# One joint tile for the rounded and low activations, and a 512-column matmul in the second mixer's gate

## The chip, the cores and the metric

The kernel runs on one NeuronCore of a Trainium2 chip. The metric is device time in microseconds (us) of one execution. The engines are named as in the profile: PE is TensorE's matmul unit and PEld its weight loads, DVE is VectorE, ACT is ScalarE, POOL is GpSimd, and SP is the queue that issues most of the DMAs.

## The reference

Two layers over 256 tokens of width 2048. The first is an RWKV-7 mixer, the second an attention mixer with three branches (compressed, selected, windowed) of 16 heads. What the change touches is the second mixer's output gate: the last 2048 columns of its input projection, z, go through silu and multiply the attention's result ahead of the output projection.

```python
def nsa_mixer(u, shared, w_in, gate_b, w_o):
    proj = u @ w_in
    q = rope_partial(proj[..., :NSA_WIDTH].reshape(B, T, H, d), jnp.arange(T))
    gl = proj[..., NSA_WIDTH:NSA_WIDTH + N_BRANCH * H] + gate_b
    z = proj[..., NSA_WIDTH + N_BRANCH * H:]
...
    o = o * jax.nn.silu(z)
    return o @ w_o
```

Here u is the RMS-normed hidden state. Weights and activations are float32.

## The kernel before, in words

Every large product is made of three matmuls on rounded numbers. A float32 tensor is split in two: a high part, rounded to fp32r by an ACT copy, and a low part, the remainder, by a subtraction. The product is high by high, high by low and low by high, all summed in one PSUM bank.

**Activations.** The activations are kept transposed, as 16 blocks k of 128 channels by T = 256 tokens. The function `ring` hands out the two tiles of a block, `mh` (high) and `ml` (low), from two rings of 16 slots each; ring 0 serves v, k, y and ob, ring 1 serves w, a, z, r and u. Each pair is written by ACT (high) and DVE or POOL (low): in `split_into` for the first mixer's mixed inputs, in `turn_y` for its result, in `turn_h` for u, and in `flush` for ob, the gated attention result. The dictionary `mixed` maps (name, k) to the pair.

**Weights.** The class `Weights` loads them in pieces of 512 KB (`wraw`, five buffers) through the SP queue, and splits them into units of 128x512: ACT writes `whi` (L204), DVE or POOL writes `wlo` (L189). Of the last 144 units of the second mixer's input projection, every third low half is POOL's. When a unit is taken, the next three have been split as well (`AHEAD` is 3).

**Two kinds of products.** In `rows_step` (L567, L568, L570) the activations are the stationary operand and up to 512 weight columns stream past; it serves v, z, the projections' outputs, the keys and values, and the queries. In `cols_step` (L585 to L587) 128 weight columns are stationary and the 256 tokens of a block stream past, so that the result is transposed, with channels on the partitions; it serves the first mixer's keys and receptance (`phase_k`, `stream`), its low-rank inputs, and the second mixer's gate. A step of k is three matmuls of 256 columns:

```python
PE.matmul(o, wh[:, s, :], mh, start=k == 0 and first, stop=False, **kw)
PE.matmul(o, wh[:, s, :], ml, start=False, stop=False, **kw)
PE.matmul(o, wl[:, s, :], mh, start=False, stop=k == NK - 1, **kw)
```

**The second mixer's stage.** The list `QZ` orders 5 blocks of queries (`phase_q`) and 16 gate heads (`phase_z`, the second function of that name). A gate head runs `cols_block` over 16 blocks k into half a PSUM bank (three banks in turn), then DVE multiplies the sum by `RST`, the row's reciprocal norm, into `zT` (L1461), ACT takes a tanh (L1463), and DVE makes silu's value out of it (L1464). Beside it runs attention as a background generator (`attn_all`, `attend`, `weigh`), a pair of heads at a time: scores, softmax on DVE and ACT, transposes of the probabilities on PE (L232 is the line of the helper that gives attention's matmuls a priority), and the products with the values. ACT copies a pair's result to `og` (L1580, one buffer); `flush` multiplies it by `zT` on POOL (L1594) and splits it into `ob` (L1596 on ACT, L1597 on POOL).

**After it.** `phase_bo` is the output projection. Its first block of 512 columns takes the blocks of `ob` downwards, k = 15 first, in `rows_step`. `open_fin` then releases the attention's memory and loads the final gain (L1622) and the residual (L1624) over the SP queue; `accumulate` (L1630) uses them after the first block.

**Order.** The program's order comes from the generators and their costs in ns (`Sched`). A scheduler then orders each engine's queue by a timeline and places the semaphore waits by the tiles' readers and writers. The start of the kernel and the recurrent scan are written out by hand in a fixed order instead.

Of the kernel before, what the change touches and what calls it, by code (L numbers as in the profile page):

```python
# [11 lines left out]
F32R = mybir.dt.float32r  # L12
AF = mybir.ActivationFunctionType
OP = mybir.AluOpType
AX = mybir.AxisListType
PSUM = bass.MemoryType.PSUM

T, D, NK = 256, 2048, 16
# [197 lines left out]
def hybrid_kernel(ctx: ExitStack, tc: tile.TileContext, a: dict, out: bass.AP):  # L216
    nc = tc.nc
    V, S, G, PE = nc.vector, nc.scalar, nc.gpsimd, nc.tensor
# [35 lines left out]
    def accp(name="acc"):  # L254
        n = turn.get(name, 0)
        turn[name] = n + 1
        b = role[name]
        return psum.tile([128, 512], F32, name=f"bank{b[n % len(b)]}", bufs=1)
# [26 lines left out]
    for q in range(4):  # L285
        for k in (4 * q, 4 * q + 2):
            first, second = [W.add(wv[(k + i) * 128:(k + i + 1) * 128, 0:1024].rearrange("p (u c) -> p u c", u=2), 1, False)
                             for i in range(2)]
# [46 lines left out]
    mixp = ctx.enter_context(tc.tile_pool(name="mixp", bufs=1))  # L335
# [63 lines left out]

    RINGS = {"v": 0, "k": 0, "y": 0, "ob": 0, "w": 1, "a": 1, "z": 1, "r": 1, "u": 1}  # L400
    owners = ([], [])
    used = set()

    def ring(nm, k):
        i = RINGS[nm]
        h = mixp.tile([128, T], F32R, name=f"mh{i}", bufs=NK)
        l = mixp.tile([128, T], F32R, name=f"ml{i}", bufs=NK)
        owners[i].append((nm, k))
        return h, l

    def ring_free(nm):
        o = owners[RINGS[nm]]
# [2 lines left out]
    def split_into(src, nm, k):  # L415
        h, l = ring(nm, k)
        S.activation(h, src, AF.Copy)  # L417
        V.tensor_tensor(l, src, h.bitcast(F32), op=OP.subtract)  # L418
        mixed[(nm, k)] = (h, l)

    def mixed_in(nm, k):
        m = ph1.tile([128, T], F32, name="mtmp", bufs=3)
        mu = MU[{"r": 0, "k": 1, "v": 2, "z": 3, "w": 4, "a": 5}[nm]]
        V.scalar_tensor_tensor(m, xx[:, k, :], mu[:, k:k + 1], xn[:, k, 1:], op0=OP.mult, op1=OP.add)  # L424
        return m
# [34 lines left out]
    if True:  # L460
# [28 lines left out]
        for k in range(2):  # L489
            norm_x(k, px[:, 256 * k:256 * k + 256], V)  # L490
            m = mixed_in("v", k)
# [64 lines left out]
    def need(key):  # L556
        if key not in mixed:
            sch.require(lambda: key in mixed)
        return mixed[key]
# [20 lines left out]
    def cols_step(o, nm, q, first=True, **kw):  # L580
        wh, wl = W.get()
        for s in range(4):
            k = 4 * q + s
            mh, ml = need((nm, k))
            PE.matmul(o, wh[:, s, :], mh, start=k == 0 and first, stop=False, **kw)  # L585
            PE.matmul(o, wh[:, s, :], ml, start=False, stop=False, **kw)  # L586
            PE.matmul(o, wl[:, s, :], mh, start=False, stop=k == NK - 1, **kw)  # L587
            yield 3 * N256

    def cols_block(nm, o):  # L590
        for q in range(4):
            yield from cols_step(o, nm, q)
# [10 lines left out]
    def phase_v():  # L603
        ps = [two() for _ in range(3)]
        lo = accp("lora")
        for q in range(4):
            for k in range(4 * q, 4 * q + 4):
                for nb in ((0, 1, 2), (2, 0, 1))[k % 2]:
                    yield from rows_step(ps[nb], "v", k, W.get(), 512)
            for i, nm in enumerate(("w", "a")):  # L610
                yield from cols_step(lo[:LORA, i * T:(i + 1) * T], nm, q, first=i == 0, skip_group_check=True)
                used.update((nm, k) for k in range(4 * q, 4 * q + 4))
        S.activation(hw, lo[:LORA, 0:T], AF.Tanh)
        S.activation(ha, lo[:LORA, T:], AF.Copy)
        for nb in range(3):
            store_v(nb, ps[nb])
        ps = two()
        yield from rows_block(ps, "v", 512, last=True)
        store_v(3, ps)
        phase_done.add("v")  # L620
# [4 lines left out]
    def phase_z(nb):  # L625
        ps = two()
        yield from rows_block(ps, "z", 512)
        for tt in range(2):
            th = kph.tile([128, 512], F32, name="zth", bufs=2)
            S.activation(th, ps[tt], AF.Tanh, scale=0.5)  # L630
            S.activation(th, th, AF.Copy, scale=0.5, bias=0.5)
            V.tensor_tensor(th, ps[tt], th, op=OP.mult)
            store_heads(zd, nb, tt, th, nc.sync)
# [255 lines left out]
    for nm, i in ZK:  # L889
        sch.run((phase_z3() if i == 3 else phase_z(i)) if nm == "z" else phase_k(i))  # L890
# [213 lines left out]
    def turn_y(U):  # L1104
        yt = [PBK[U][:, x * 512:x * 512 + 256] for x in range(2)]
        for i in range(NCH):
            for x, h in each:
                r = H(x, h)
                PE.matmul(yt[x][R[h], i * 64:i * 64 + 64], OU[U][r, x, i, :], ident[r, r], start=True, **mm)
        made = [ring("y", 2 * U + x) for x in range(2)]  # L1110
        for x, (yh, yl) in enumerate(made):
            S.activation(yh, yt[x], AF.Copy)
            mixed[("y", 2 * U + x)] = (yh, yl)
        for x, (yh, yl) in enumerate(made):
            V.tensor_tensor(yl, yt[x], yh.bitcast(F32), op=OP.subtract)
        sch.t += 350
# [137 lines left out]
    def turn_h(nb, xl):  # L1254
        for kp in range(2):
            pt = accp("tp")
            for i in range(2):
                for tt in range(2):
                    PE.transpose(pt[:, i * 256 + tt * 128:i * 256 + tt * 128 + 128],
                                 xl[:, tt, (2 * kp + i) * 128:(2 * kp + i + 1) * 128], ident)  # L1260
            sch.t += 430
            for i in range(2):
                k = nb * 4 + 2 * kp + i
                src = pt[:, i * 256:i * 256 + 256]
                for nm, gg in (("kv", KVG), ("u", BG)):
                    if nm == "u":
                        h, l = ring(nm, k)
                    else:
                        h = kvp.tile([128, T], F32R, name="kvh", bufs=NK)
                        l = kvp.tile([128, T], F32R, name="kvl", bufs=NK)  # L1270
                    S.activation(h, src, AF.Copy, scale=gg[:, k:k + 1])
                    V.scalar_tensor_tensor(l, src, gg[:, k:k + 1], h.bitcast(F32), op0=OP.mult, op1=OP.subtract)
                    mixed[(nm, k)] = (h, l)
# [146 lines left out]
    RST = at.tile([128, T], F32, name="RST")  # L1420
# [33 lines left out]
            qd[h0 + g] = (qh, ql)  # L1454

    def phase_z(h):
        o = accp("acc")[:, :T]
        yield from cols_block("u", o)
        sch.require(lambda: h + ZB >= HEADS or ("ob", h + ZB) in mixed)
        z = at.tile([128, T], F32, name="zT", bufs=ZB)  # L1460
        V.tensor_tensor(z, o, RST, op=OP.mult)  # L1461
        th = at.tile([128, T], F32, name="zth", bufs=2)
        S.activation(th, z, AF.Tanh, scale=0.5)  # L1463
        V.scalar_tensor_tensor(z, th, 1.0, z, op0=OP.add, op1=OP.mult)  # L1464
        zdone[h] = z
# [146 lines left out]
    for ph in QZ:  # L1612
        sch.run(phase_q(ph) if ph < 10 else phase_z(ph - 10))
# [91 lines left out]
```

## Time and profile before

| | us |
|---|---|
| median of 3 runs | 1187.53 |
| lowest, highest run | 1182.65, 1189.38 |
| span of the profiled execution, first to last instruction | 1181.0 |
| second mixer's stage, queries, attention and gate | 855 to 1087 |
| output projection and final norm | 1087 to 1181 |

The profile gives the profiled execution's span, not its whole time; the median of the runs lies 6.5 us above that span. In the profile's rows "x16" is a count, the number behind the bar is the busy time in us and then the mean duration of one in ns, and the part behind the second bar is the engine's idle time ahead of the group with what ended it. An output and its inputs stand as out<-in. In the rows in order of time the first number is the start and the second the duration, both in us. Matmuls overlap each other, so their durations add up to more than the time they take.

### The profile page before, as it was taken

Reading aid. Unit: us, or ns where it says so; the run is one execution under the profiler, and the core shown is the slowest. Engines: PE = TensorE matmul, PEld = TensorE weight load, DVE = VectorE, ACT = ScalarE, POOL = GpSimd, SP = SyncE. Lnnn points to the kernel's source line nnn. Section 1 sums busy time; section 2 is a strip of 40 time slices with the busy share of each in tenths; the row PEclk is TensorE's granted clock in tenths of the full one; section 3 lists DMA queues with packets and bytes.
Section 4 is the critical chain, followed back from the end, with each engine's and each line's share of the span. In section 5 each row is a group of like instructions: output and inputs, shape, how many; then the busy total and the mean of one; then the engine's idle time right before and its main releaser. Section 6 shows DMA issues by size and latency. Waiting matters only on the chain.

```text
span 1181.0 us, 25607 instructions
## 1 busy us (share of the span) xinstructions
PE 1130.3 (96%) x9416; PEld 985.4 (83%) x9416; DVE 851.3 (72%) x1915; ACT 710.8 (60%) x1680; POOL 330.9 (28%) x413
## 2 busy tenths in 40 slices
PE   8999999999986999999989999999999999999997
PEld 7788899887965888888668888787989989989887
DVE  6999876589794876666655867674576888786564
ACT  5767777666762345565445867564656657665553
POOL 1300046234454255654000010100333233333011
PEclk8999999999997999999999999999999999999999
DMA  6558887786888669685355758585645353644752
GB/s 227 173 181 256 219 224 227 224 215 187 263 236 190 174 173 262 175 220 152 106 169 206 247 163 294 164 285 164 190 131 157 107 138 112 164 104 160 289 195 105
DMA packets 232765, 225.26 MB, mean 191 GB/s; under 512 B 51344, under 2 KB 180672, under 8 KB 232256
## 3 DMA queue, kind: packets, MB, share of 16 engines
q1 hardware_dynamic: 228000, 219.01, 61.8%
q0 software_dynamic: 4640, 4.62, 1.6%
q8 instruction: 74, 1.21, 0.4%
q14 instruction: 51, 0.42, 0.1%
HBM read 200.48 MB, written 23.10 MB: 189 GB/s over the span
## 4 chain that ended last, share of the span: by engine, by line
PE 76%; DVE 12%; DMA 4%; issue 4%; ACT 3%; POOL 2%; SPq 0%; ACTq 0%; POOLq 0%; DVEq 0%
PE bank L568 12%; PE bank L567 12%; PE bank L570 12%; PE bank L585 8%; PE bank L586 6%; PE bank L587 6%; PE bank L232 5%; DVE wlo L189 4%; PE pair L570 1%; PE pair L567 1%; PE pair L568 1%; DVE mtmp L424 1%; DVE ml L418 1%; PE pair L1046 1%; DVE invX L794 1%
## 5 line engine op out<-in xcount | busy, mean ns | idle before, releaser
L189 DVE TENSOR_TENSOR wlo<-wraw,whi 128x512 fp32r<-128x512 f32 (+2 forms) x616 | 441.9, 730 | 151.4 <-ACT whi L204 149.0
L204 ACT ACTIVATE whi<-wraw 128x512 fp32r<-128x512 f32 (+2 forms) x664 | 402.3, 619 | 199.3 <-PE bank L570 96.6
L585 PE MATMUL bank<-mh,whi 128*128 128x256 f32 (+1 forms) x800 | 239.7, 300 | 0.7 <-issue 0.7
L568 PE MATMUL bank<-wlo,mh 128*128 128x512 f32 (+3 forms) x608 | 230.2, 380 | 4.2 <-DVE wlo L189 4.2
L587 PE MATMUL bank<-mh,wlo 128*128 128x256 f32 (+1 forms) x800 | 228.6, 286 | 1.7 <-DVE wlo L189 1.7
L586 PE MATMUL bank<-ml,whi 128*128 128x256 f32 (+1 forms) x800 | 228.7, 286 | 0.0
L570 PE MATMUL bank<-whi,ml 128*128 128x512 f32 (+3 forms) x608 | 228.5, 378 | 0.0
L567 PE MATMUL bank<-whi,mh 128*128 128x512 f32 (+3 forms) x608 | 204.4, 381 | 0.9 <-ACT whi L204 0.9
L585 PEld LDWEIGHTS bank<-mh,whi 128*128 128x128 f32 (+1 forms) x800 | 152.3, 190 | 6.5 <-issue 0.9
L587 PEld LDWEIGHTS bank<-mh,wlo 128*128 128x128 f32 (+1 forms) x800 | 152.3, 191 | 3.2 <-DVE wlo L189 2.0
L586 PEld LDWEIGHTS bank<-ml,whi 128*128 128x128 f32 (+1 forms) x800 | 152.8, 191 | 2.2 <-issue 0.8
L568 PEld LDWEIGHTS bank<-wlo,mh 128*128 128x128 f32 x608 | 115.1, 189 | 22.5 <-DVE wlo L189 5.1
L567 PEld LDWEIGHTS bank<-whi,mh 128*128 128x128 f32 x608 | 114.6, 190 | 20.1 <-ACT whi L204 1.3
L570 PEld LDWEIGHTS bank<-whi,ml 128*128 128x128 f32 x608 | 114.8, 189 | 17.8 <-issue 0.4
L189 POOL TENSOR_TENSOR wlo<-wraw,whi 128x512 fp32r<-128x512 f32 (+2 forms) x48 | 62.6, 1305 | 190.1 <-ACT whi L204 158.3
L568 PE MATMUL bank<-wlo,kvh 128*128 128x512 f32 x192 | 77.0, 401 | 0.0
L570 PE MATMUL bank<-whi,kvl 128*128 128x512 f32 x192 | 76.1, 396 | 0.0
L567 PE MATMUL bank<-whi,kvh 128*128 128x512 f32 x192 | 67.4, 396 | 0.0
L417 ACT ACTIVATE mh<-mtmp 128x256 fp32r<-128x256 f32 x96 | 38.9, 413 | 27.2 <-DVE mtmp L424 25.6
L424 DVE SCALAR_TENSOR_TENSOR mtmp<-xx,prm,xn 128x256 f32<-128x256 f32 x96 | 47.8, 510 | 1.2 <-POOL xx L456 1.0
L715 POOL TENSOR_TENSOR sp<-an,pinv 64x256 f32<-64x256 f32 x32 | 36.3, 1133 | 34.1 <-DVE an L710 32.6
L1035 ACT ACTIVATE X<-pair 128x128 f32<-128x128 f32 x32 | 8.9, 279 | 58.5 <-PE pair L1033 35.9
(325 smaller groups left out, 1909.3 us busy)
## 6 DMA issues: line engine op xcount, KB each, us to landing
wraw<-in_a_w_rkvz_dram SPq DMA_DIRECT2D x128, 512.0 KB, 4.9
wraw<-in_kv_w_dram SPq DMA_DIRECT2D x48, 512.0 KB, 4.5
wraw<-in_b_w_in_dram SPq DMA_DIRECT2D x40, 512.0 KB, 4.0
wraw<-in_a_w_o_dram SPq DMA_DIRECT2D x32, 512.0 KB, 4.1
wraw<-in_b_w_o_dram SPq DMA_DIRECT2D x32, 512.0 KB, 3.7
spd<-sp SPq DMA_DIRECT2D x16, 642.0 KB, 4.7
spl<-spd SPq DMA_DIRECT2D x16, 642.0 KB, 5.6
wraw<-in_b_w_in_dram SPq DMA_DIRECT2D x24, 384.0 KB, 3.2
```

What stands on the lines that cost most here:

```text
L189: eng.tensor_tensor(lv, src, hv.bitcast(F32), op=OP.subtract)
L204: self.nc.scalar.activation(hv, src, AF.Copy)
L232: return fn(*args, **kw)
L417: S.activation(h, src, AF.Copy)
L424: V.scalar_tensor_tensor(m, xx[:, k, :], mu[:, k:k + 1], xn[:, k, 1:], op0=OP.mult, op1=OP.add)
L567: PE.matmul(o, mh[:, ts], wh[:, 0, :], start=k == ends[0], stop=False)
L568: PE.matmul(o, mh[:, ts], wl[:, 0, :], start=False, stop=False)
L570: PE.matmul(o, ml[:, ts], wh[:, 0, :], start=False, stop=k == ends[1])
L585: PE.matmul(o, wh[:, s, :], mh, start=k == 0 and first, stop=False, **kw)
L586: PE.matmul(o, wh[:, s, :], ml, start=False, stop=False, **kw)
L587: PE.matmul(o, wl[:, s, :], mh, start=False, stop=k == NK - 1, **kw)
L715: G.tensor_tensor(BK[r, :, h, :], c3(an)[r], c3(pinv)[r], op=OP.mult)
```

## The change: a joint tile, and one wide matmul for the high weights

`ring` now allocates one tile of 128 x 2 x 256 for a block's high and low activations and returns its halves, for every name of both rings. Where the gate calls `cols_step`, it passes a whole bank of 512 columns; the high weights then take both halves as one 512-column matmul, and the low weights take the high half into the bank's first 256 columns. At the last k the low weights come first, so that the wide matmul closes the sum. `phase_z` adds the bank's two halves with a reduction on DVE, which reads PSUM with a stride, and multiplies by `RST` on POOL. All other callers of `cols_step` keep their three matmuls of 256 columns.

```diff
     owners = ([], [])
+    joint = {}
     used = set()
 
     def ring(nm, k):
         i = RINGS[nm]
-        h = mixp.tile([128, T], F32R, name=f"mh{i}", bufs=NK)
-        l = mixp.tile([128, T], F32R, name=f"ml{i}", bufs=NK)
+        m = mixp.tile([128, 2, T], F32R, name=f"mx{i}", bufs=NK)
         owners[i].append((nm, k))
-        return h, l
+        joint[nm, k] = m
+        return m[:, 0, :], m[:, 1, :]
...
             mh, ml = need((nm, k))
-            PE.matmul(o, wh[:, s, :], mh, start=k == 0 and first, stop=False, **kw)
-            PE.matmul(o, wh[:, s, :], ml, start=False, stop=False, **kw)
-            PE.matmul(o, wl[:, s, :], mh, start=False, stop=k == NK - 1, **kw)
+            if o.shape[1] == T:
+                PE.matmul(o, wh[:, s, :], mh, start=k == 0 and first, stop=False, **kw)
+                PE.matmul(o, wh[:, s, :], ml, start=False, stop=False, **kw)
+                PE.matmul(o, wl[:, s, :], mh, start=False, stop=k == NK - 1, **kw)
+            else:
+                end = k == NK - 1
+                if not end:
+                    PE.matmul(o, wh[:, s, :], joint[nm, k], start=k == 0, stop=False, **kw)
+                PE.matmul(o[:, :T], wl[:, s, :], mh, start=False, stop=False, **kw)
+                if end:
+                    PE.matmul(o, wh[:, s, :], joint[nm, k], start=False, stop=True, **kw)
             yield 3 * N256
...
     def phase_z(h):
-        o = accp("acc")[:, :T]
+        o = accp("acc")
         yield from cols_block("u", o)
         sch.require(lambda: h + ZB >= HEADS or ("ob", h + ZB) in mixed)
         z = at.tile([128, T], F32, name="zT", bufs=ZB)
-        V.tensor_tensor(z, o, RST, op=OP.mult)
+        V.tensor_reduce(z, o.rearrange("p (a t) -> p t a", a=2), axis=AX.X, op=OP.add)
+        G.tensor_tensor(z, z, RST, op=OP.mult)
```

## The prediction

> **What bounds the kernel now.** I read the profile page first, then the busy times by stage, then the second mixer's stage alone: groups by form, PE's waits, and the instructions in order of time.
>
> ```profile
> span 1181.0 us, 25607 instructions
> PE 1130.3 (96%) x9416; PEld 985.4 (83%) x9416; DVE 851.3 (72%) x1915; ACT 710.8 (60%) x1680; POOL 330.9 (28%) x413
> PE 76%; DVE 12%; DMA 4%; issue 4%; ACT 3%; POOL 2%; SPq 0%; ACTq 0%; POOLq 0%; DVEq 0%
> L585 PE MATMUL bank<-mh,whi 128*128 128x256 f32 (+1 forms) x800 | 239.7, 300 | 0.7 <-issue 0.7
> ...
> core 0: us, PE busy (x) PEld busy (x) DVE busy (x) ACT busy (x) POOL busy (x), PEclk, DMA share, GB/s
> 855.00:1087.00 232.00, 231.09 (x1566) 213.16 (x1566) 177.34 (x488) 147.38 (x421) 79.76 (x72) 1.00 0.47 133
> ...
> 940.00:960.00 20.00, 20.00 (x127) 19.09 (x126) 17.57 (x53) 13.45 (x41) 7.66 (x8) 1.00 0.47 128
> ...
> PE bank L1449 <- DVE qt L1308: 0.9, 1, 0.9
> ```
>
> The second and third lines say that TensorE (PE) is busy 96% of the span and holds 76% of the chain that ended last. The stage of the change, 855 to 1087 us, is PE's more than any: 231.09 of 232 us busy, the granted clock at 1.00, and the last line is all that the view of waits gives for PE in this stage, 0.9 us once. VectorE (DVE) has room there (177.34 us, densest 17.57 of 20), GpSimd (POOL) much room (79.76 us). So what a matmul costs PE there is paid in the end time, and what DVE and POOL do there is paid only if PE comes to wait for it.
>
> A matmul's duration is no price, since matmuls overlap; the price is the distance from one start to the next. The start times below are from four stretches: the gate alone; a 512-column matmul of attention between gate matmuls; and the output projection and the key and value pass, whose 512-column matmuls follow each other.
>
> ```profile
> start us, us, engine line op out<-in xcount [idle before <-releaser]
> 1080.41 0.28 PE L585 MATMUL bank<-mh,whi 128*128 128x256 f32 x1
> ...
> 1084.37 0.28 PE L585 MATMUL bank<-mh,whi 128*128 128x256 f32 x1
> ...
> 1029.84 0.40 PE L232 MATMUL bank<-Th,vh 128*128 128x512 f32 x1
> 1030.07 0.28 PE L586 MATMUL bank<-ml,whi 128*128 128x256 f32 x1
> 1030.19 0.28 PE L587 MATMUL bank<-mh,wlo 128*128 128x256 f32 x1
> ...
> 1089.74 0.39 PE L568 MATMUL bank<-wlo,mh 128*128 128x512 f32 x1
> ...
> 1091.33 0.39 PE L570 MATMUL bank<-whi,ml 128*128 128x512 f32 x1
> ...
> 759.71 0.40 PE L570 MATMUL bank<-whi,kvl 128*128 128x512 f32 x1
> ...
> 762.51 0.40 PE L570 MATMUL bank<-whi,kvl 128*128 128x512 f32 x1
> ```
>
> Between the first two rows lie eleven steps of three matmuls: 3.96 us / 33 = 120 ns for a 256-column matmul. Between 1089.74 and 1091.33 lie seven distances: 227 ns for 512 columns. In the key and value pass, 759.71 to 762.51, it is 2.80 us / 12 = 233 ns. Between gate matmuls the 512-column one took 230 ns to the next start, and the 256-column one behind it 120: mixing the sizes costs nothing extra. Doubling the columns adds 107 ns, so each 256-column matmul carries about 13 ns that don't depend on its columns.
>
> **The change part by part.** *The gate's matmuls.* Sixteen heads by sixteen blocks k are 256 steps. (L585's 800 are the keys' and receptance's 256 each, these 256 and 32 for the low-rank products.) A step was 3 x 120 = 360 ns; it becomes 227 + 120 = 347. That removes 256 matmuls and 256 weight loads and saves 256 x 13 = 3.3 us. The bounds: with the 233 ns of the key and value pass the step is 353 and the saving 1.8 us; below, if the long matmul took twice the short one, 240, nothing is saved. I take 227, because there a mixed tile meets a weight piece as in the gate (with the roles of stationary and moving operand exchanged), and the 230 of the gate's own stage lies beside it. The last step's other order (low weights first) changes no count, and its low weights belong to the same piece of four blocks as its high ones.
>
> The Trainium skill, page "TensorE: Matmul & The Clock Gate", section "Back-to-back issue gap", puts the gap of warm isolated matmuls at N/2.4 + 2.5 ns. By that rule a step would go from 327.6 to 325.1 ns and the change would save 0.6 us; the trace differs, with 120 and 227 where the rule has 109 and 216, and the measurement decides.
>
> *Reading the sum.* These rows are the stage's groups by form:
>
> ```profile
> L1461 DVE TENSOR_TENSOR zT<-bank,RST 128x256 f32<-128x256 f32 x16 | 6.7, 418 | 9.8 <-PE bank L587 9.8
> L1506 DVE TENSOR_REDUCE mx<-bank 128x2 f32<-128x512 f32 x16 | 10.9, 684 | 0.0
> L1594 POOL TENSOR_TENSOR og<-og,zT 128x256 f32<-128x256 f32 x16 | 13.4, 841 | 37.1 <-ACT og L1580 20.0 <-DVE zT L1464 12.9 <-DVE rc L1525 2.6
> L189 POOL TENSOR_TENSOR wlo<-wraw,whi 128x512 fp32r<-128x512 f32 x25 | 37.1, 1484 | 75.2 <-ACT whi L204 48.7 <-PE bank L587 10.8 <-DVE bank L1502 4.5
> L1464 DVE SCALAR_TENSOR_TENSOR zT<-zth,zT 128x256 f32<-128x256 f32 x16 | 8.2, 514 | 0.5 <-ACT zth L1463 0.5
> ```
>
> The multiply of 418 ns on DVE becomes a reduction of 512 elements; the nearest row is L1506's 684 ns, which also reads 512 out of PSUM but writes 2 results, not 256. Bounds: 418, if the result count sets the time, and twice 684, if the stride of 256 elements costs. I take 684: 16 x 0.27 = 4.3 us more on DVE (0 to 15). The multiply moves to POOL, at L1594's shape: 16 x 0.84 = 13.5 us. Neither engine is the stage's bound: DVE goes from 177 to 182 of 232 us, POOL from 80 to 93. Each head's gate is ready later by 0.27 + 0.84, about 1.1 us. Who waits for that:
>
> ```profile
> 1078.67 0.60 ACT L1580 ACTIVATE og<-bank 128x512 f32<-128x512 f32 x1 [2.48 <-PE bank L232]
> ...
> 1084.93 0.42 DVE L1461 TENSOR_TENSOR zT<-bank,RST 128x256 f32<-128x256 f32 x1 [0.21 <-PE bank L587]
> ...
> 1086.58 0.74 POOL L1594 TENSOR_TENSOR og<-og,zT 128x256 f32<-128x256 f32 x1 [2.64 <-DVE zT L1464]
> 1087.84 0.77 POOL L1597 TENSOR_TENSOR ml<-og,mh 128x256 fp32r<-128x256 f32 x1 [0.53 <-ACT mh L1596]
> ...
> 1088.63 0.34 SPq L1622 DMA_DIRECT2D fg<-in_final_g_dram  x1
> 1089.03 0.43 SPq L1624 DMA_DIRECT2D h<-hd  x1
> ```
>
> The last head ends its chain at 1088.61 (third and fourth row). The output projection takes the blocks downwards from 15, six matmuls of 227 ns each, from about 1084.9 on, so block 1 is due 14 x 1.36 = 19 us later, at 1104: 15 us of cover for 1.1 us. The loads of the final gain and the residual (SP's queue) start when the attention's buffers are released by that last POOL operation, and the weights of the projection queue behind them; they come 1.1 us later against PE, while the residual is first used after the first block of columns, 16 x 1.36 = 22 us in. The attention result's buffer is single; its copy (first row) waited for PE, not for the gate. So these costs are covered, and I charge nothing; if a cover were gone it would be 1.1 us once at the end.
>
> *New waits.* POOL's multiply waits for DVE's reduction, which waits for the head's last matmul. Behind it on POOL stand low weight halves (L189, 1484 ns) and the multiply of attention's result; behind the reduction on DVE, other low halves and the softmax. PE waits for the halves, but when a piece is taken the next three are split as well, so a half is asked for some four pieces ahead, 4 x 4 x 0.347 = 5.6 us of PE's work, against 0.68 + 0.84 + 1.48 = 3.0 us for the new chain and one half behind it.
>
> *The joint tile* holds the same bytes and the same two writers. A slot is now reused when both halves have been read; the two last reads are neighbours on PE, 0.12 to 0.23 us apart. The queue orders outside the stages written out by hand are built anew from these dependencies, so they can shift a little anywhere: no price, spread only.
>
> *The sum:* 1181.0 - 3.3 = 1177.7 us of span, and I give back 0.3 for shifts. The median of the runs, 1187.5, lies 6.5 above the profiled span; the same distance puts the forecast at 1184.5 us. The three runs spread over 6.7 us, so 0.5% (5.9 us) is about what a measurement can tell from no change; the forecast lies within.
>
> **The rivals.**
> *The saving is swallowed.* PE's gaps below a few hundred ns are hidden in its overlapping durations; where PE is paced by attention's short transposes and their copies, 3.3 us less filler only widens the gaps. For it: DVE at 17.57 of 20 us in the densest stretch. Against it: one wait of 0.9 us in 232. It gives 1187.5 to 1188.
>
> *POOL holds the weights up* (slower). Place: the z multiply on POOL with a low half behind it. If the half is the next piece that PE needs (1.4 us of cover, not 5.6), PE stands 3.0 - 1.4 = 1.6 us; from the point where every second head meets this, 8 x 1.6 = 13 us are lost and 3.3 won: 1197. For it: POOL already stood 12.9 us behind zT and 10.8 us behind the gate's matmuls, with halves queued. Against it: PE never waited for a half in the stage.
>
> *The tile's new place in memory* (slower). The 227 and 233 ns of 512 columns have the same clock and engine; the rows differ in the stationary tiles' names, so their place could be the reason. If the joint tiles fell on the bad side, the row passes on mixed tiles would pay:
>
> ```profile
> L567 PE MATMUL bank<-whi,mh x608: 278/389/797, 15.5 to 1161.2; 128*128 128x512 f32 x112, 128*128 128x384 f32 x24, 128*128 128x432 f32 x8, 128*128 128x256 f32 x8
> L567 PE MATMUL pair<-whi,mh x64: 386/390/497, 569.7 to 648.6; 128*128 128x512 f32 x64
> ```
>
> The first row gives the forms of a quarter of its 608; 112 of 152 are 512 wide, so 448 of all, and with the pairs' 64 it is 512, on each of three lines (L567, L568, L570). 1536 by 6 ns are 9.2 us, less the 3.3 saved: 1193.4. It decides only if place matters at all, which no row separates.
>
> *Other orders.* The rebuilt queue orders gain or lose more than the arithmetic: 6 us or so to either side, 1178 or 1193.
>
> *Columns are nearly free* (much faster). If a 512-column matmul cost little over a 256-column one, a step would fall to about 240 ns: 256 x 120 = 31 us, 1157. The measured 227 against 120 speak against it. The same page of the Trainium skill and the same section give 131 ns for 512 columns and 81 for 128 in a stream with weight loads; between them, as an estimate, 98 for 256, and 16.6 us saved; the trace's 227 disagrees.
>
> **How the numbers follow.** Forecast 0.55, swallowed 0.15, POOL 0.08, tile's place 0.08, other orders 0.12 (half each way), free columns 0.02. Faster by over 0.5%: 0.02, 0.05 of the orders, 0.04 from the forecast's runs by their spread: 0.11. Slower: 0.07 of POOL, 0.06 of the place, 0.05 of the orders: 0.18. The rest, 0.71, is within. The range 1178 to 1193.5 takes in the unknown prices (0 to 3.3 us saved), the runs' spread and most of the orders and the place, and leaves out POOL and free columns.
>
> **What would show it.** Right: 256 matmuls and loads fewer; in the gate's undisturbed stretch a step of 347 ns (11 steps in 3.8 us, not 3.96); the reduction near 0.68 us; PE's waits in the stage still near 1 us; the stage 2 to 4 us shorter and the others unchanged. Wrong: steps of 360 or 240; PE waiting for low halves of POOL; 512-column matmuls of the output projection at 233; or a stage ahead of the gate that changed its length by more than 3 us.

## The result, and the profile after

| | us |
|---|---|
| after, median of 13 runs (lowest, highest) | 1180.75 (1178.37, 1183.66) |
| before, 13 runs beside them | 1187.53 (1182.65, 1191.29) |
| ratio, with its 95% interval | 0.9948 (0.9933 to 0.9962) |
| after, profiled execution: span, whole time | 1181.6, 1183.66 |

The changed kernel is faster by about 6 us, 0.52%. The two profiled spans, 1181.0 and 1181.6, hide this: the profiled execution of before is one of its quickest, that of after is its slowest. So stages are compared below inside the profiles, and the whole by the runs. A run's time is its span and about 2 us. One run of before beside the experiments e1 to e4 took 3771.61 us; the median of 1187.82 below is over 29 runs with it, the 98 runs further below are without it.

**The gate's stage.** First the page of the kernel after, then its 855 to 1087 us by stage (PE, PEld, DVE, ACT, POOL busy, then granted clock), then all of PE's waits there.

```profile
PE 1133.4 (96%) x9160; PEld 975.2 (83%) x9160; DVE 861.1 (73%) x1915; ACT 711.4 (60%) x1680; POOL 344.5 (29%) x429
```

```profile
855.00:1087.00 232.00, 231.51 (x1333) 202.50 (x1332) 190.11 (x499) 149.76 (x427) 93.48 (x86) 1.00 0.50 137
```

```profile
PE bank L569 <- DVE wlo L189: 0.3, 1, 0.3
PE bank L232 <- DVE ql L1462: 0.2, 1, 0.2
```

256 matmuls and 256 weight loads are gone. PE is as dense as before (231.51 of 232 us), and waits 0.5 us in all: none of the new waits reached it. DVE and POOL each took on about 13 us. Where those went, by groups of the same window:

```profile
L593 PE MATMUL bank<-mx,whi 128*128 128x512 f32 x240 | 87.0, 398 | 0.0
L594 PE MATMUL bank<-mx,wlo 128*128 128x256 f32 x256 | 70.7, 285 | 0.0
...
L1471 POOL TENSOR_TENSOR zT<-zT,RST 128x256 f32<-128x256 f32 x16 | 14.2, 891 | 31.0 <-DVE zT L1470 31.0
...
L1470 DVE TENSOR_REDUCE zT<-bank 128x256 f32<-128x512 f32 x16 | 10.9, 682 | 2.1 <-PE bank L596 1.9
```

The reduction takes 682 ns, 0.26 us more than the multiply that it replaces, which makes 4.2 of DVE's 13 us; low weight halves (L189) are another 4.3 us in this window, and the rest is spread over attention's operations. The price of the matmuls is again the distance between starts:

```profile
1079.98 0.40 PE L593 MATMUL bank<-mx,whi 128*128 128x512 f32 x1
1080.21 0.28 PE L594 MATMUL bank<-mx,wlo 128*128 128x256 f32 x1
1080.33 0.39 PE L593 MATMUL bank<-mx,whi 128*128 128x512 f32 x1
```

The step is 350 ns: 233 from the wide matmul to the narrow one, 117 back (medians over the undisturbed steps of the stage). It was 360, so 256 steps save 2.6 us. That is less than half of what the runs show.

**The rest is at and after the hand-over to the scan** (the first mixer's recurrence), near 350 us, where no line of the change computes. The joint tile's dependencies let the scheduler order the queues there otherwise. SP's queue of the kernel before, in order of time, then of the kernel after:

```profile
349.84 0.37 SPq L176 DMA_DIRECT2D wraw<-in_a_w_rkvz_dram  x1
350.26 4.15 SPq L874 DMA_DIRECT2D spl<-spd  x2
354.50 0.54 SPq L754 DMA_DIRECT2D invA<-abd  x1
355.13 7.14 SPq L852 DMA_DIRECT2D Yb<-yvd  x8
362.31 3.61 SPq L754 DMA_DIRECT2D invA<-abd  x7
```

```profile
347.23 6.06 SPq L883 DMA_DIRECT2D spl<-spd  x2
353.38 0.93 SPq L763 DMA_DIRECT2D invA<-abd  x2
354.40 5.81 SPq L861 DMA_DIRECT2D Yb<-yvd  x8
360.26 3.08 SPq L763 DMA_DIRECT2D invA<-abd  x6
363.44 0.43 SPq L176 DMA_DIRECT2D wraw<-in_a_w_rkvz_dram  x1
```

A load of weights that stood ahead of the scan's first loads (spl, Yb) now stands behind them. Around it some matmuls, weight splits, mixes and stores change places on the other engines too. PE's longest wait of the program, for Yb, fell with it (before, then after):

```profile
PE pair L967 <- DMA Yb<-yvd: 13.5, 4, 11.8
```

```profile
PE pair L976 <- DMA Yb<-yvd: 11.7, 4, 10.0
```

The half clock that follows the pause lasts 17.1 us before and 13.7 after, by the trace's record of the granted clock.

### The profile page after: what moved, and what is told of

Read it like the earlier page. It is cut to its first block, busy times and chain, and to the rows that moved or that the text cites. A ratio compares the mean times of both kernels' runs of the same rounds, so it can differ in the third digit from the quotient of the medians.

```text
span 1181.6 us, 25078 instructions
## 1 busy us (share of the span) xinstructions
PE 1133.4 (96%) x9160; PEld 975.2 (83%) x9160; DVE 861.1 (73%) x1915; ACT 711.4 (60%) x1680; POOL 344.5 (29%) x429
## 4 chain that ended last, share of the span: by engine, by line
PE 75%; DVE 11%; DMA 4%; issue 3%; ACT 3%; POOL 2%; SPq 1%; ACTq 0%; POOLq 0%; DVEq 0%
PE bank L569 12%; PE bank L568 12%; PE bank L571 12%; PE bank L232 5%; PE bank L593 5%; PE bank L587 4%; PE bank L589 3%; PE bank L588 3%; DVE wlo L189 3%; PE bank L594 3%; PE pair L571 1%; PE pair L568 1%; PE pair L569 1%; DMA invA<-abd 1%; ACT whi L204 1%
## 5 line engine op out<-in xcount | busy, mean ns | idle before, releaser
L189 DVE TENSOR_TENSOR wlo<-wraw,whi 128x512 fp32r<-128x512 f32 (+2 forms) x616 | 442.8, 732 | 145.9 <-ACT whi L204 142.2
L569 PE MATMUL bank<-wlo,mx 128*128 128x512 f32 (+3 forms) x608 | 230.1, 380 | 5.2 <-DVE wlo L189 5.2
L571 PE MATMUL bank<-whi,mx 128*128 128x512 f32 (+3 forms) x608 | 228.5, 378 | 0.0
L568 PE MATMUL bank<-whi,mx 128*128 128x512 f32 (+3 forms) x608 | 204.1, 379 | 1.2 <-ACT whi L204 1.1
L587 PE MATMUL bank<-mx,whi 128*128 128x256 f32 (+1 forms) x544 | 167.1, 307 | 0.3 <-ACT mx L418 0.3
L589 PE MATMUL bank<-mx,wlo 128*128 128x256 f32 (+1 forms) x544 | 156.2, 288 | 0.6 <-DVE wlo L189 0.6
L588 PE MATMUL bank<-mx,whi 128*128 128x256 f32 (+1 forms) x544 | 156.0, 287 | 0.0
L569 PEld LDWEIGHTS bank<-wlo,mx 128*128 128x128 f32 x608 | 114.8, 189 | 24.4 <-DVE wlo L189 6.7
L568 PEld LDWEIGHTS bank<-whi,mx 128*128 128x128 f32 x608 | 114.1, 189 | 19.9 <-ACT whi L204 1.5
L571 PEld LDWEIGHTS bank<-whi,mx 128*128 128x128 f32 x608 | 114.7, 189 | 17.5
L189 POOL TENSOR_TENSOR wlo<-wraw,whi 128x512 fp32r<-128x512 f32 (+2 forms) x48 | 62.4, 1301 | 168.2 <-ACT whi L204 135.5
L587 PEld LDWEIGHTS bank<-mx,whi 128*128 128x128 f32 (+1 forms) x544 | 104.2, 192 | 5.7 <-ACT mx L418 0.7
L589 PEld LDWEIGHTS bank<-mx,wlo 128*128 128x128 f32 (+1 forms) x544 | 104.4, 192 | 1.9 <-DVE wlo L189 1.0
L588 PEld LDWEIGHTS bank<-mx,whi 128*128 128x128 f32 (+1 forms) x544 | 104.8, 193 | 0.9
L593 PE MATMUL bank<-mx,whi 128*128 128x512 f32 x240 | 87.0, 398 | 0.0
L594 PE MATMUL bank<-mx,wlo 128*128 128x256 f32 x256 | 70.7, 285 | 0.0
```

The source lines that it names most:

```text
L189: eng.tensor_tensor(lv, src, hv.bitcast(F32), op=OP.subtract)
L568: PE.matmul(o, mh[:, ts], wh[:, 0, :], start=k == ends[0], stop=False)
L569: PE.matmul(o, mh[:, ts], wl[:, 0, :], start=False, stop=False)
L571: PE.matmul(o, ml[:, ts], wh[:, 0, :], start=False, stop=k == ends[1])
L593: PE.matmul(o, wh[:, s, :], joint[nm, k], start=k == 0, stop=False, **kw)
L594: PE.matmul(o[:, :T], wl[:, s, :], mh, start=False, stop=False, **kw)
```

## The experiments

Each ran with the kernel before on the same chip, 12 runs of its own (e3 six); the ratio is to those runs of before, whose medians were 1187.82, 1188.12 and 1189.11 us in the three sets (e1 to e4, e5 to e8, e9 to e12).

### e1: the joint tile alone

```diff
 def ring(nm, k):
-    h = mixp.tile([128, T], F32R, name=f"mh{i}", bufs=NK)
-    l = mixp.tile([128, T], F32R, name=f"ml{i}", bufs=NK)
+    m = mixp.tile([128, 2, T], F32R, name=f"mx{i}", bufs=NK)
...
-    return h, l
+    return m[:, 0, :], m[:, 1, :]
```

> The joint tile for both rings, but the gate as before: three 256-column matmuls a step and DVE's multiply. Theory A (two sources: 2.6 us from the gate's wide matmul, and some 3.5 us from the rebuilt order around the hand-over to the scan, 330 to 366 us, which comes from the joint tile's dependencies): about 3.5 us faster than before, ratio 0.997, and the orders of ACT, DVE and PE differ from before only around 330 to 366 us, as in the changed kernel. Rival B (all of the gain is made in the gate's stage): ratio 1.000. Rival C (the tile's new place in memory moves the matmuls' pace): the 512-column matmuls of the output projection no longer at 227 ns, or 256-column steps no longer at 120.

1183.56 us, ratio 0.9961 (0.9947 to 0.9976). Without any wide matmul 4.3 us of the gain are there. So the gain has two sources. The pause for Yb is 10.0 us, with 13.7 us of half clock behind it, as after.

### e2, e3: the kernel before and the changed kernel once more

> The kernel before, once more. All theories: ratio 1.000 within its interval. Its profile is a second sample of the hand-over and of the granted clock in the scan: theory A expects PE's longest pause there, 12.2 us in the first profile, to stay above the changed kernel's 10.4; a theory of chance expects it anywhere between 10 and 13.

> The changed kernel, once more, beside the others on one chip. All theories: ratio 0.993 to 0.997. Theory A: from the first residual addition to the last instruction its profile is some 2.6 us shorter than before, and what else it gains lies ahead of 400 us. Rival B: the whole 6 us lie in 855 to 1107 us.

e2: 1189.05 us, 1.0015 (0.9994 to 1.0037). e3: 1181.41 us, 0.9948 (0.993 to 0.9967), the first result again. The wide matmuls' part is the distance from e1 to e3, 2.2 us by the medians; between the profiles, from the first residual addition of the first mixer to the end, the time is 537.0 us before, 538.0 in e1, 534.4 after and 534.8 in e3.

### e4: the multiply by RST back on DVE

```diff
-        G.tensor_tensor(z, z, RST, op=OP.mult)
+        V.tensor_tensor(z, z, RST, op=OP.mult)
```

> The changed kernel with the multiply by the row norm on DVE (16 x 0.42 us more there) and not on POOL (16 x 0.89 us less). If both are covered by PE's work, as the prediction had it: the same time as the changed kernel within 0.15%, PE's waits in the stage still below 2 us. Rival (DVE is near its limit in the stage): 3 to 7 us slower than the changed kernel. Rival (POOL's chain costs PE something now): 1 to 4 us faster.

1182.32 us, 0.9959 (0.9943 to 0.9975): 0.9 us over e3, within what the two intervals leave open. POOL costs nothing that shows, and moving the multiply there gains little. (From the first residual addition to the end e4 has 537.1 us, with 3.4 us at half clock at 949 us, where after and e3 have none.)

### e5: the joint tile for ring 0 alone

```diff
 def ring(nm, k):
     i = RINGS[nm]
+    if i == 0:
+        m = mixp.tile([128, 2, T], F32R, name=f"mx{i}", bufs=NK)
...
+        return m[:, 0, :], m[:, 1, :]
```

> The joint tile for ring 0 alone (v, k, y and the second mixer's ob); ring 1 keeps two tiles of 128x256 per block, and the gate keeps its three narrow matmuls. Every engine's order of instructions is then the one of the kernel before. Theory A1 (the joint tile gains through the orders that it changes at the hand-over to the scan): 1.000 of before, within 0.002, TensorE's long pause near 350 us stays at 12 to 13.2 us, and the half clock after it lasts five windows (17.07 us). Rival D (the joint tile gains by itself, through fewer tiles to allocate, free and wait for, whatever the order): about half of the 4.3 us or more, 0.998 or less, as ring 0 holds half of the blocks.

1188.38 us, 0.9993 (0.9969 to 1.0017), pause 12.0 us, 17.1 us of half clock. Half of the joint tiles, but DVE, ACT, POOL and SP keep the order of before throughout: nothing is gained. That speaks for the order and against the tile. Ring 1's tiles were not run in the old order.

### e6, e7: the one weight load by itself

```diff
-            self.nc.sync.dma_start(v, ap)
+            if self.loaded == 109:
+                with self.tc.issue_after(self.yb.ins):
+                    self.nc.sync.dma_start(v, ap)
+            else:
+                self.nc.sync.dma_start(v, ap)
```

That is e6, made on the kernel before; `yb` is the last load of Yb. e7 is made on e1, with this line in place of the third:

```diff
+                with self.tc.high_priority(offset=2000):
```

> The kernel before, with one change: one of the weight loads on SP's queue (the one that stands just ahead of the loads of spl, invA and Yb at the hand-over to the scan) is issued behind the last load of Yb, as it stands in the kernel with the joint tile. The orders of the other engines stay as before. Theory A1, in its narrow form (SP's order alone does it): ratio 0.996 to 0.998, TensorE's pause about 10.4 us, four windows of half clock after it (13.65 us). Theory A2 (the changed orders of ScalarE, VectorE or GpSimd there do it): 1.000, a pause of 12 us or more. Rival D: 1.000, as there is no joint tile.

> The joint tile for both rings with the narrow gate, and that one weight load raised in priority, so that it is issued on SP between the two loads of spl, ahead of invA and Yb, much as in the kernel before. The orders of the other engines are those of the joint tile alone. A1: the gain of the joint tile goes: 0.999 to 1.001 with a pause of 12 us or more. A2 and D: 0.996 as the joint tile alone had, with a pause of 10 to 10.5 us.

e6: 1184.69 us, 0.9978 (0.9955 to 1.0001). e7: 1184.30 us, 0.9965 (0.9942 to 0.9988). Neither form of the theory holds as it was put. Moving the one load gains 3.4 us by the medians and 2.6 by the ratio (its interval just reaches none), yet the pause stays at 12.3 us. Putting it back among the joint tile's orders leaves the gain, with a pause of 10.7. So the load seems to be one way to a gain and the orders of the other engines another, and the pause's length is not the measure of it.

### e8: the keys in the wide form too

```diff
-        S.activation(ksb, pk, AF.Copy)
-        S.activation(sqk, pk, AF.Square, scale=KK[:, j:j + 1])
+        V.tensor_reduce(ksb, pk.rearrange("p (a t) -> p t a", a=2), axis=AX.X, op=OP.add)
+        S.activation(sqk, ksb, AF.Square, scale=KK[:, j:j + 1])
...
-        o = kacc[0][:, (j % 2) * 256:(j % 2) * 256 + 256]
+        o = accp("acc")
```

> The changed kernel, with the first mixer's keys in the same form as the gate: a whole bank for each block of columns, high weights against both halves as one 512-column matmul (256 of them), and VectorE sums the halves into ksb where ScalarE copied (16 reductions of about 0.68 us for 16 copies of 0.38 us; the square then reads ksb). By the spacings measured in the gate (350 ns for 360 a step) 256 steps save 2.6 us of TensorE between 150 and 327 us. Theory E (TensorE is the bound there, as it is in the gate): 0.9925 to 0.9935 of before, 2 to 2.6 us under the changed kernel. Rival F (the reduction stands ahead of the key chain and VectorE also splits the weights there; or the transfers, which use 0.7 to 0.9 of the DMA engines, set the stage's pace): no gain or a loss of up to 3 us on the changed kernel, with new idle time of TensorE at the weights or at the key chain.

1182.50 us, 0.9952 (0.993 to 0.9974): no gain on the changed kernel. The rows of the key chain's first matmul, after and then e8 (shortest, median and longest ns, then first and last start in us), and e8's waits of PE from 330 to 420 us:

```profile
L677 PE MATMUL bank<-hw,w2s x32: 377/379/454, 132.7 to 315.6; 96*128 96x256 f32 x32
```

```profile
L677 PE MATMUL bank<-hw,w2s x32: 377/378/381, 132.2 to 311.7; 96*128 96x256 f32 x32
```

```profile
PE pair L973 <- DMA Yb<-yvd: 14.7, 3, 13.9
PE bank L589 <- DVE wlo L189: 2.0, 2, 1.7
```

The key stage did end 3.9 us earlier (0.5 of it was there at its start), and PE then stood 13.9 us for Yb where it had stood 10.0. PE's saving ahead of a wait for loads is given back in that wait.

### e9 to e12: the scan's first Yb loads ahead of the large ones

```diff
-                for x in range(2):
-                    nc.sync.dma_start(SPL0[x][:, :SPW], spd[x])
-                load_y(0, nc.sync)
+                W.yb = load_y(0, nc.sync).ins
+                with tc.issue_after(W.yb):
+                    for x in range(2):
+                        nc.sync.dma_start(SPL0[x][:, :SPW], spd[x])
...
-                nc.sync.dma_start(A[u0:u0 + 16], src)
+                with tc.issue_after(W.yb) if b else ExitStack():
+                    nc.sync.dma_start(A[u0:u0 + 16], src)
```

The same edit on the kernel before, on e1, on the changed kernel and on e8.

> The kernel before, with the eight loads of Yb (16 KB each) ahead of the two loads of spl (642 KB each) and of invA on SP's queue; the other engines' orders stay. In the kernel before TensorE stands 12.2 us at the hand-over to the scan, until the first Yb has landed. Theory P (that pause, set by the queue, is where the joint tile gained): the pause falls to 2 to 6 us, and the time by 5 to 10 us, 0.992 to 0.996 of before, with fewer half-clock windows behind the pause (two to four for five). Rival Q (the loads put behind are late next: spl and invA land 5 us later, and the idle time only moves): 0.999 to 1.002, with new waits of TensorE, VectorE or GpSimd on spl between 365 and 385 us.

> The same order of loads on the joint tile alone (narrow gate). Theory P: the joint tile's gain came through this pause, so that it is spent here: within 1.5 us of the kernel before with Yb first. Rival R (the joint tile gains at other places, in the clock or in the scan, whatever the pause): 3 to 5 us under the kernel before with Yb first, as it was without that order.

> The same order of loads on the changed kernel. By every theory the gate's 2.6 us are under the joint tile with Yb first. P: 0.988 to 0.992 of before, 4 to 8 us under the changed kernel. Q: as the changed kernel, 0.9948.

> The same order of loads on the kernel with the keys in the wide form too. There the last load into the keys' chain ended 5 us earlier than in the kernel before, and TensorE's pause at the hand-over grew to 14.1 us for it. Theory P: with the pause cut the keys' saving comes through: 2 to 5 us under the changed kernel with Yb first. Q: as the kernel with wide keys had, 0.995 of before.

| run | us | ratio to before (95%) |
|---|---|---|
| e9, on before | 1188.36 | 0.9994 (0.9972 to 1.0016) |
| e10, on the joint tile | 1185.06 | 0.9972 (0.995 to 0.9995) |
| e11, on the changed kernel | 1183.67 | 0.9963 (0.9939 to 0.9986) |
| e12, on e8 | 1184.04 | 0.9962 (0.9945 to 0.9979) |

The theory of the pause falls: it is shorter in all four (PE's matmuls stand 6.5, 6.3, 5.8 and 8.7 us apart there, for 12.2, 10.4, 10.4 and 14.1), and none is faster for it. PE's waits of e9 and of e10 from 340 to 440 us:

```profile
PE pair L970 <- DMA Yb<-yvd: 6.9, 3, 6.1
PE bank L587 <- DVE wlo L189: 6.3, 1, 6.3
PE bank L1005 <- DVE mb L959: 1.9, 1, 1.9
PE pair L1036 <- DVE S L1057: 1.3, 1, 1.3
```

```profile
PE pair L971 <- DMA Yb<-yvd: 6.4, 2, 5.9
PE bank L588 <- DVE wlo L189: 6.4, 1, 6.4
PE bank L1006 <- DVE mb L960: 1.9, 1, 1.9
PE pair L1044 <- DVE sta L1074: 0.7, 1, 0.7
PE pair L1037 <- DVE S L1058: 0.4, 1, 0.4
```

The second line is what came late next. DVE's queue of e9 in order of time shows why:

```profile
370.00 0.18 DVE L761 COPY invT<-invA 128x16 f32<-128x16 f32 x1 [17.48 <-DMA uv<-vd]
...
372.76 0.68 DVE L189 TENSOR_TENSOR wlo<-wraw,whi 128x512 fp32r<-128x512 f32 x1
```

The queue is fixed in this stage. Its next instruction reads invA (the matrices that DVE inverts for the scan); DVE stood 17.5 us for its loads, and the weight half that PE needs stood behind it. (The view names uv, which landed last of what it saw; the copy reads invA, loaded on the same queue just ahead.) The rival that PE's idle time only moves was right, though to DVE's invA, not to spl.

This wait of DVE is not new in e9. The same row in before, in e10 and in e1:

```profile
370.30 0.18 DVE L760 COPY invT<-invA 128x16 f32<-128x16 f32 x1 [17.10 <-DMA uv<-vd]
371.77 0.18 DVE L762 COPY invT<-invA 128x16 f32<-128x16 f32 x1 [17.26 <-DMA uv<-vd]
369.17 0.19 DVE L761 COPY invT<-invA 128x16 f32<-128x16 f32 x1 [14.25 <-DMA invA<-abd]
```

In before it lay hidden behind PE's wait for Yb, and it is this one that sets the end of the hand-over: from the copy's start to the end of PE's later wait for DVE's mb (1.9 us in every profile) are 16.4 us in twelve of the fourteen profiles, and 16.6 in the two with wide keys. DVE is busy in 15.1 of these us in before and in e1 alike. From the end of DVE's last instruction ahead of its wait to that same point, the hand-over takes 33.5, 33.8, 32.9 and 33.8 us in before, e2, e5 and e9, 30.6 in e1, and 30.2, 29.8 and 29.7 in after, e3 and e4. So about 3 us of the joint tile's gain are made here, where invA reaches DVE sooner. e6 and e7 have 32.8 and 32.0. With Yb first it is 33.6 on the joint tile, 32.6 on the changed kernel and 32.8 on e8, which alone had 31.6: that order brings the hand-over most or all of the way back to the length of before. Which of the moved instructions lets invA come sooner is not shown.

There is a second part. e9 and e10 have the same two long waits, within 0.2 us each by the longest, and the same hand-over, and e10 is still 3.3 us faster by the medians (2.5 by the means, with a 95% interval of about 0.3 to 4.6). So some of the joint tile's gain is made behind the hand-over. The last lines above are where the two differ: PE waits 1.3 us for the scan's state S in e9, 0.4 in e10.

### What the fourteen profiles have in common

That wait, near 427 us, is in before, e2, e5 and e9, and in none of the ten others, where S costs 0.5 us or less. The four have the old orders on every engine but for e9's SP; e6 has them on every engine but SP too, and is among the ten. In e5 and then in e1, PE's waits from 418 to 446 us:

```profile
PE pair L1037 <- DVE S L1058: 1.3, 1, 1.3
PE pair L1044 <- DVE sta L1074: 0.7, 1, 0.7
```

```profile
PE pair L1041 <- DVE sta L1071: 0.7, 1, 0.7
PE pair L1034 <- DVE S L1055: 0.4, 1, 0.4
```

The difference of 0.9 us may stand for more. The stretch from 426 to 444 us by stage, in e2, in e9 and in e1 (the granted clock is the third number from the end):

```profile
426.00:444.00 18.00, 16.00 (x247) 14.33 (x247) 12.23 (x31) 9.70 (x28) 5.06 (x9) 0.72 0.42 133
```

```profile
426.00:444.00 18.00, 17.01 (x324) 15.11 (x324) 12.04 (x30) 8.80 (x27) 5.18 (x9) 0.81 0.42 120
```

```profile
426.00:444.00 18.00, 17.21 (x344) 15.19 (x343) 14.62 (x36) 9.70 (x28) 8.19 (x15) 1.00 0.58 147
```

PE executes 247 and 324 matmuls there at a clock of 0.72 and 0.81, and 344 at 1.00. (e1 has its wait for S before the stretch, at 424 us, so the stretches are not quite the same work.) In e2, e5 and e9 the half clock lasts 10.2, 10.2 and 6.8 us from 428 to 431 us on. Before's own profiled execution has the wait and no half clock behind it (it was a quick one); of the ten others one, after, has 3.4 us there. Another piece of 3.4 us, near 453 to 461 us, tells nothing: seven profiles of both kinds have it.

The runs without a trace agree. For each run the granted clock is known as a mean over its span, and span x (1 - clock) is the time lost to it:

| kernel | runs | mean clock | lost, us | rest of the span, us |
|---|---|---|---|---|
| before, all three sets | 98 | 0.9823 | 21.0 | 1165.3 |
| e5 (old orders) | 12 | 0.9823 | 21.0 | 1165.6 |
| e9 (old orders, Yb first) | 12 | 0.9818 | 21.6 | 1164.6 |
| e6 (one load moved) | 12 | 0.9837 | 19.2 | 1164.4 |
| e7 (joint, load put back) | 12 | 0.9844 | 18.4 | 1163.8 |
| e10 (joint) | 12 | 0.9844 | 18.4 | 1164.8 |
| e1 (joint) | 12 | 0.9837 | 19.3 | 1162.5 |
| after | 13 | 0.9843 | 18.5 | 1160.7 |

The means carry 0.2 to 1.1 us of standard error each. The kernels with the wait for S lose 21 to 23 us to the clock (e2, not in the table, 23.0), the others 18 to 20.5 (e8 20.1 and e12 20.5 the most). Between e9 and e10 the lost time differs by 3.2 us and the rest by 0.2, so as far as these means tell, what sets the two apart goes with the clock. Between before and after 2.5 us are lost time, and the rest fell by 4.6: 2.6 for the gate's matmuls, and about 2 for shorter waits. The two columns are no separate causes at the hand-over: it is 3.3 us shorter in after's profile, and it also has one piece of 3.41 us at half clock less, which counts as 1.7 us of lost time though PE waits for DVE at its end in either kernel.

## Why the prediction was right, and where it was off

The direction and the range were right: 1180.75 lies in 1178 to 1193.5. The forecast of 1184.5 had somewhat under half of the gain, 3.0 us of 6.8 by the medians, and the mechanism of that half; the other part came from a term that it had put at nothing.

- **The gate's step** was put at 347 ns, bounds to 353; it is 350. The 512-column matmul took the 233 ns of the key and value pass, not the 227 of the output projection; the 256-column one came 3 ns earlier than its 120. So 2.6 us, not 3.3. The rule of the Trainium skill's page "TensorE: Matmul & The Clock Gate", section "Back-to-back issue gap", would have saved 0.6; the trace shows 10 ns a step where it has 2.5.
- **The reduction** was priced at 684 ns from a row with two results and measured 682 with 256: neither the stride nor the number of results shows. POOL's multiply was put at 0.84 us and takes 0.89.
- **Covers and waits** held: 0.5 us of PE's waits in the stage, and e4, with the multiply on DVE, is no faster. POOL did stand 31.0 us for the reduction, and PE did not see it.
- **The joint tile, "no price, spread only"**, is the term that was mis-sized. It is worth 4.3 us by e1, more than the matmuls. The prediction had the cause, queue orders built anew, and gave it as a rival of about 6 us to either side with a chance of 0.12, half of it a gain; in the sum it stood as 0.3 us given back, with the wrong sign. One of the prediction's own signs of being wrong, a change of more than 3 us ahead of the gate, is met at the hand-over (3.3 us). The sign could not be had from the trace of before. The size could have been taken more seriously: in that trace PE already stood 13.5 us for Yb, DVE 17.1 us for invA, and PE waited for S, behind queues that are ordered by dependencies.
- **The rivals.** "Swallowed" fell in the gate, and e8 shows the same saving swallowed in the key stage, where a wait for loads follows. "POOL holds the weights up" did not occur. "The tile's new place" fell: the output projection's 512-column matmuls stand 227 ns apart (median) in before, e1 and after alike. "Columns nearly free" fell at 233 against 117.
- **The 6.5 us around the span** were no fixed cost. 2 us are; the rest was a quick profiled execution, and adding it back was right only since it puts the forecast on the median.

Shown is that the gain outside the gate comes with the joint tile's dependencies and without any wide matmul (e1); that it does not come where the queues keep their order (e5, for ring 0's tiles); that PE's wait for Yb does not set it (e9: 6 us shorter, nothing gained); and that the hand-over, which ends with DVE's wait for invA, is about 3 us shorter in e1, after, e3 and e4. No run shortened the wait for invA by itself. Behind the hand-over, e9 against e10 leaves some 3 us that go with the granted clock, but for e1 only about 1 us of its 4.3 is left; the runs do not settle this part more closely. That the 1.3 us wait for S is what brings on the half clock behind it is only argued, from three of four profiles that have it against one of ten that don't; against it, PE stands idle 1.2 us at 430 us in e6 (the view names no releaser), and no half clock follows. Open stays why a load moved on SP, or mixes and splits moved on the other engines, both bring DVE to S in time: DVE is 0.3 us earlier at 370 us, 0.8 at 400 and 2.5 at 426 in e6 than before, gained in small steps.

## What to carry to other kernels

Price a matmul by the distance of starts in the stretch that is most like the new one, same neighbours and same operand roles, and take the whole cost of a wide form from there: here it was 10 ns for each pair joined. A change of tiles is a change of dependencies, and where a scheduler orders the queues from those, run the tile change alone (here e1's 4.3 us were more than the arithmetic's 2.6). And before shortening a wait, look for another one that lies hidden behind it on a second engine and ends at the same place: a pause of PE cut from 12.2 to 6.5 us came back as 6.3 us, since DVE's wait for invA kept its 17 us.

## What the runs showed of the hardware

The half clock comes in pieces of 3.41 us: 17.1, 13.7, 10.2 and 6.8 are five, four, three and two of them. At the hand-over, where Yb's loads kept their place, five followed a wait for Yb of 10.7 to 13.9 us and four one of 9.3 to 10.0. So there a shorter wait went with one piece less. What that piece is worth in time is not shown, since PE waits for DVE behind it. The Trainium skill's page "TensorE: Matmul & The Clock Gate", in its Part 1 on the clock gate, gives a window of 3413 ns that runs freely and does not start with the kernel; the pieces agree with the length. That a wait of 1.3 us is followed by three pieces in one execution and by none in another would fit a free-running window, but no run here separates that from other causes. The same page of the Trainium skill, in its section "HAM oscillation — how this bites in real kernels", warns of idle gaps above about 3.4 us; these waits of 1.3 and 0.7 us, some 3.5 us apart, are shorter. Over 98 runs of the kernel before, span and granted clock go together with a correlation of -0.82: some two thirds of the span's variance go with the clock.
